# Row means by one accumulating VectorE instruction in a kernel that subtracts the mean and squares

## The chip, the cores and the metric

One core of a Trainium2 chip. The experiments ran on three such chips; each was timed in the same rounds as the kernel before, whose median was 83.1 to 83.2 us on all of them. The metric is the device time of one execution in microseconds (us). All runs were at a granted clock of 1.0. Times given are medians of several executions; a ratio is the mean time of one kernel's runs over that of the kernel before in the same rounds, so it is not quite the ratio of the two medians. The span of a profile, 81.4 us for the kernel before, is shorter than the time by some 1.8 us. A transfer is issued when the instruction that hands it to the queue starts, and has landed when the last of its 16 completion signals arrives; between landing and the first instruction that waited for it lie some 0.02 us, and the text uses either. The lead of a store is the time between its issue and the landing of the transfer ahead of it.

## The reference

```python
x = randn(1024, 4096) as float32
mean = np.mean(x, axis=-1, keepdims=True)
out  = ((x - mean) ** 2).astype(np.float32)
```

16.78 MB are read and 16.78 MB written. Each element is used for one sum, one subtraction and one product.

## The kernel before

Two tiles (i = 0, 1), each of 128 partitions x 4 rows x 4096 columns, 8.39 MB. Both loads are issued at the start. Per tile ScalarE takes the mean of row 3, VectorE those of rows 0 to 2; ScalarE squares three rows and 9/16 of another, VectorE the rest; then one store, on the same queue as the loads.

```python
    for i in range(ntiles):
        x_tile = io.tile([P, Q * D], F32)
        nc.sync.dma_start(out=x_tile, in_=x_t[i])            # load 0, load 1
        tiles.append(x_tile)
    # ... cut: helpers
    #   mean_on_act: activation(Identity, scale=-inv_d, accum_out=neg_mean)
    #   mean_on_dve: reduce_sum(negate=True), then tensor_scalar_mul by inv_d
    #   square_on_act: activation(Square, bias=neg_mean), in place
    for i in range(ntiles):
        row = [tiles[i][:, q * D:(q + 1) * D] for q in range(Q)]
        m3 = mean_on_act(row[3])
        m0 = mean_on_dve(row[0])
        square_on_act(row[3], m3)
        m1 = mean_on_dve(row[1])
        square_on_act(row[0], m0)
        m2 = mean_on_dve(row[2])
        square_on_act(row[1], m1)
        square_on_act(row[2][:, :H], m2)                     # H = 9/16 of a row
        back = row[2][:, H:]
        nc.vector.tensor_scalar_add(out=back, in0=back, scalar1=m2)
        nc.vector.tensor_mul(out=back, in0=back, in1=back)
        nc.sync.dma_start(out=out_t[i], in_=tiles[i])        # store 0, store 1
```

## Time and profile before

| What | Kernel before |
|---|---|
| time, 3 runs before the prediction | 83.25 us (83.16 to 83.27) |
| span of the profile | 81.4 us |
| VectorE, ScalarE busy | 33.4 us, 34.7 us |
| transfer queue busy | 96.0% of the span |
| loads land at | 22.7 and 42.05 us |
| stores issued at | 39.68 and 59.00 us |
| stores land at | about 61.4 and 80.7 us |

### The profile page before, as it was taken

The numbers are of one execution on the slowest core, as the hardware profiler recorded it, in microseconds if no ns is written. First come the engines' busy times: TensorE is split into PE (matmuls) and PEld (weight loads), VectorE is DVE, ScalarE is ACT, GpSimd is POOL, SyncE is SP. The second block draws the span as 40 slices with busy tenths as digits, with TensorE's granted clock in tenths as the row PEclk, the third lists the DMA queues.
The fourth block names the chain that finished last, engine by engine and source line by source line (L and its number), as shares of the span: only waits on it lengthen the run. The fifth ranks groups of instructions, "written<-read, shape, count | busy, mean of one in ns | idle before, by whom it ended". The sixth has DMA issues, their size and how long they took to land.

```text
span 81.4 us, 79 instructions
## 1 busy us (share of the span) xinstructions
DVE 33.4 (41%) x16; ACT 34.7 (43%) x13; POOL 0.2 (0%) x4
## 2 busy tenths in 40 slices
DVE  0000000000089999999439999999900000000000
ACT  6000000000089999999339999999800000000000
POOL 0000000000000000000000000000000000000000
DMA  9099956999982999992999992999997499998390
GB/s 483 32 515 515 483 258 290 515 515 515 515 386 129 515 515 515 515 451 129 451 515 515 515 483 129 418 515 515 515 515 322 193 515 515 515 515 386 161 483 0
DMA packets 577, 33.55 MB, mean 412 GB/s; under 512 B 65, under 2 KB 65, under 8 KB 65
## 3 DMA queue, kind: packets, MB, share of 16 engines
q1 hardware_dynamic: 576, 33.55, 96.0%
q14 instruction: 1, 0.00, 0.0%
HBM read 16.78 MB, written 16.78 MB: 412 GB/s over the span
## 4 chain that ended last, share of the span: by engine, by line
DMA 50%; DVE 21%; SPq 0%; issue 0%
DMA x_tile<-in_x_dram 50%; DVE neg_sum L62 16%; DVE x_tile L85 2%; DVE x_tile L84 1%; DVE neg_mean L65 1%; SPq L46 0%
## 5 line engine op out<-in xcount | busy, mean ns | idle before, releaser
L62 DVE TENSOR_REDUCE neg_sum<-x_tile 128x1 f32<-128x4096 f32 x6 | 26.5, 4413 | 25.2 <-DMA x_tile<-in_x_dram 25.2
L69 ACT ACTIVATE x_tile<-x_tile,neg_mean 128x4096 f32<-128x4096 f32 (+1 forms) x8 | 26.0, 3323 | 0.1
L54 ACT ACTIVATE copy<-x_tile 128x4096 f32<-128x4096 f32 x2 | 7.2, 3617 | 23.3 <-DMA x_tile<-in_x_dram 23.3
L85 DVE TENSOR_TENSOR x_tile<-x_tile 128x1792 f32<-128x1792 f32 x2 | 4.1, 2026 | 0.1
L84 DVE TENSOR_SCALAR x_tile<-x_tile,neg_mean 128x1792 f32<-128x1792 f32 x2 | 2.3, 1154 | 0.1
L54 ACT ACT_TABLE_LOAD x1 | 1.3, 1283 | 0.7 <-PEq L103 0.7
L65 DVE TENSOR_SCALAR neg_mean<-neg_sum 128x1 f32<-128x1 f32 x6 | 0.9, 154 | 0.2
L54 ACT ACTIVATION_READ_ACCUMULATOR copy<-x_tile 128x1 f32 x2 | 0.4, 187 | 0.0
L103 POOL MEMSET const-bfloat16-1.0<- 128x1 bf16 x1 | 0.1, 101 | 0.0
L103 POOL MEMSET const-uint8-127<- 128x1 uint8 x1 | 0.1, 101 | 0.0
L103 POOL MEMSET const-float32-0.0<- 128x1 f32 x1 | 0.1, 98 | 0.2 <-issue 0.2
L103 POOL MEMSET const-float32-1.0<- 128x1 f32 x1 | 0.1, 98 | 0.0
## 6 DMA issues: line engine op xcount, KB each, us to landing
x_tile<-in_x_dram SPq DMA_DIRECT2D x2, 31.4
out_dram<-x_tile SPq DMA_DIRECT2D x2, 21.7
```

The costliest lines, as they stand in the source:

```text
L54: nc.scalar.activation(out=copy, in_=row, func=ACT.Identity, scale=-inv_d, accum_out=neg_mean)
L62: inorder(nc.vector.reduce_sum(out=neg_sum, in_=row, axis=mybir.AxisListType.X, negate=True))
L65: inorder(nc.vector.tensor_scalar_mul(out=neg_mean, in0=neg_sum, scalar1=inv_d))
L69: inorder(nc.scalar.activation(out=part, in_=part, func=ACT.Square, bias=neg_mean, scale=1.0))
L84: nc.vector.tensor_scalar_add(out=back, in0=back, scalar1=m2)
L85: nc.vector.tensor_mul(out=back, in0=back, in1=back)
L103: nc = _bacc.Bacc("TRN2", target_bir_lowering=False, num_devices=1)
```

## The change

Its intent: less VectorE time per mean. One instruction adds the left half of a row to its right half (2048 pairs), scales and accumulates, and so gives minus the mean directly. ScalarE no longer takes means, and VectorE squares only 1/8 of every fourth row.

```diff
-        m3 = mean_on_act(row[3])
-        m0 = mean_on_dve(row[0])
-        square_on_act(row[3], m3)
         ... (all means and squares of the tile)
+        for q in range(Q):
+            row = tiles[i][:, q * D:(q + 1) * D]
+            pairs = scratch.tile([P, HALF], F32)
+            neg_mean = stats.tile([P, 1], F32)
+            inorder(nc.vector.tensor_tensor_reduce(
+                out=pairs, in0=row[:, :HALF], in1=row[:, HALF:],
+                scale=-inv_d, scalar=0.0, op0=ADD, op1=ADD, accum_out=neg_mean))
+            cut = D if q < Q - 1 else LAST                   # LAST = 7/8 of a row
+            nc.scalar.activation(out=row[:, :cut], in_=row[:, :cut],
+                                 func=ACT.Square, bias=neg_mean, scale=1.0)
+            if cut < D:
+                rest = row[:, cut:]
+                nc.vector.tensor_scalar_add(out=rest, in0=rest, scalar1=neg_mean)
+                nc.vector.tensor_mul(out=rest, in0=rest, in1=rest)
         nc.sync.dma_start(out=out_t[i], in_=tiles[i])
```

More of the change, by code (lines that the diff above doesn't have):

```diff
@@ L12 @@
 ACT = mybir.ActivationFunctionType
+ADD = mybir.AluOpType.add
 @with_exitstack
@@ L30 @@
     Q = 4
-    H = D * 9 // 16
+    HALF = D // 2
+    LAST = D - D // 8
     assert B % (P * Q) == 0
@@ L40 @@
     scratch = ctx.enter_context(tc.tile_pool(name="scratch", bufs=1))
-    stats = ctx.enter_context(tc.tile_pool(name="stats", bufs=2 * ntiles * Q))
+    stats = ctx.enter_context(tc.tile_pool(name="stats", bufs=ntiles * Q))
     tiles = []
@@ L49 @@
     inorder = tc.keep_in_program_order
-    def mean_on_act(row):
-        copy = scratch.tile([P, D], F32)
-        neg_mean = stats.tile([P, 1], F32)
-        nc.scalar.activation(
-            out=copy, in_=row, func=ACT.Identity, scale=-inv_d, accum_out=neg_mean
-        )
-        return neg_mean
-    def mean_on_dve(row):
-        neg_sum = stats.tile([P, 1], F32)
-        neg_mean = stats.tile([P, 1], F32)
-        inorder(nc.vector.reduce_sum(
-            out=neg_sum, in_=row, axis=mybir.AxisListType.X, negate=True
-        ))
-        inorder(nc.vector.tensor_scalar_mul(out=neg_mean, in0=neg_sum, scalar1=inv_d))
-        return neg_mean
@@ L68, in square_on_act @@
-    def square_on_act(part, neg_mean):
-        inorder(nc.scalar.activation(
-            out=part, in_=part, func=ACT.Square, bias=neg_mean, scale=1.0
-        ))
-    for i in range(ntiles):
-        row = [tiles[i][:, q * D:(q + 1) * D] for q in range(Q)]
-        m3 = mean_on_act(row[3])
-        m0 = mean_on_dve(row[0])
-        square_on_act(row[3], m3)
-        m1 = mean_on_dve(row[1])
-        square_on_act(row[0], m0)
-        m2 = mean_on_dve(row[2])
-        square_on_act(row[1], m1)
-        square_on_act(row[2][:, :H], m2)
-        back = row[2][:, H:]
-        nc.vector.tensor_scalar_add(out=back, in0=back, scalar1=m2)
-        nc.vector.tensor_mul(out=back, in0=back, in1=back)
+    for i in range(ntiles):
+        for q in range(Q):
[3 more added lines that the diff above has]
+            inorder(nc.vector.tensor_tensor_reduce(
+                out=pairs,
+                in0=row[:, :HALF],
+                in1=row[:, HALF:],
+                scale=-inv_d,
+                scalar=0.0,
+                op0=ADD,
+                op1=ADD,
+                accum_out=neg_mean,
+            ))
+            cut = D if q < Q - 1 else LAST
+            nc.scalar.activation(
+                out=row[:, :cut],
+                in_=row[:, :cut],
+                func=ACT.Square,
+                bias=neg_mean,
+                scale=1.0,
+            )
+            if cut < D:
+                rest = row[:, cut:]
+                nc.vector.tensor_scalar_add(out=rest, in0=rest, scalar1=neg_mean)
+                nc.vector.tensor_mul(out=rest, in0=rest, in1=rest)
```

## The prediction

Passages that no trace or run shows are cut from the text below, and the cuts are marked. Some were terms of its sum, estimates: how the time of the new instruction was reckoned (some 2.3 us, which with 0.154 us for the read makes the 2.45 us a row), the 1.2 us for the tail of 512 columns, and a delay of up to 0.25 us behind the table load, without which store 0 comes at 39.4 rather than "39.4 to 39.7". With them the sum came to 11.0 us a tile for VectorE and 14.1 for ScalarE, both stores issued 0 to 0.3 us earlier, and 83.2 us. In the half-rate rival, where the instruction takes about twice as long (some 4.4 us), the 18.3 us for four rows is such a term too. That rival was the prediction's main doubt, as the trace of the kernel before has no instruction that accumulates over two inputs. The prediction set the product against it, which took 2026 ns for 1792 pairs, 1.13 ns a pair; the reduction beside it took 4413 ns for 4096 single values, 1.08 ns a value.

> **What bounds the kernel now.** I read the page first, then time order, then the waits. The kernel moves 16.78 MB in and 16.78 MB out in four transfers of 8.39 MB: load 0, load 1, store 0, store 1. The page says how busy everyone is:
>
> ```profile
> DVE 33.4 (41%) x16; ACT 34.7 (43%) x13; POOL 0.2 (0%) x4
> ...
> q1 hardware_dynamic: 576, 33.55, 96.0%
> ...
> HBM read 16.78 MB, written 16.78 MB: 412 GB/s over the span
> ```
>
> Each computing engine rests more than half of the 81.4 us span, while the transfer queue is busy 96% of it. A busy share is an average over stages, so I cut the span at the times when transfers land: 22.7 and 42.05 (the first compute of each tile starts there, having waited for a load), then 61.4.
>
> ```profile
> 22.70:42.05 19.35, 16.71 (x8) 16.72 (x6) 0.00 (x0) 1.00 1.00 434
> 42.05:61.40 19.35, 16.71 (x8) 16.72 (x6) 0.00 (x0) 1.00 1.00 434
> ```
>
> The columns are the stretch, its length, DVE, ACT and POOL busy time, PE clock, DMA share, GB/s. In both stretches each engine needs 16.7 us, the transfers need all 19.35 us, and their rate is the same 434 GB/s. In the first stretch load 1 moves while tile 0 is computed; in the second store 0 moves while tile 1 is computed. So compute lies beside a transfer both times.
>
> What matters is when the stores are issued, which is where compute could hold up the queue:
>
> ```profile
> 39.68 19.67 SPq L86 DMA_DIRECT2D out_dram<-x_tile  x2
> ...
> 42.05 3.62 ACT L54 ACTIVATE copy<-x_tile 128x4096 f32<-128x4096 f32 x1 [2.59 <-DMA x_tile<-in_x_dram]
> ...
> 45.80 13.01 ACT L69 ACTIVATE x_tile<-x_tile,neg_mean 128x4096 f32<-128x4096 f32 x4
> ...
> 56.91 2.03 DVE L85 TENSOR_TENSOR x_tile<-x_tile 128x1792 f32<-128x1792 f32 x1
> 59.00 0.34 SPq L86 DMA_DIRECT2D out_dram<-x_tile  x1
> ```
>
> Store 0 is issued at 39.68 us, 2.4 us before load 1 lands. Store 1 is issued at 59.00. The view of the transfers gives 21.6 to 21.7 us from issue to landing for a store, so store 0 lands at about 61.4 and store 1 at about 80.7. Store 0 thus lands 19.35 us after load 1, and store 1 lands 19.3 us after store 0: the pure streaming time of 8.39 MB, with no room for a gap. Each store is in the queue before the one ahead of it has drained. The chain of work that ended last lists VectorE between 42.05 and 59.0, but it follows what released the last issue. It doesn't say that the issued transfer then waited about 2.4 us for its turn. **The transfers bound every stage: four times 19.35 us is 77.4, about 3.3 us of start come ahead (load 0 lands at 22.7 rather than 19.35) and 0.7 of ending after 80.7, which makes the 81.4.**
>
> [...] The trace has a load of 1283 ns and 3698 for the squares.
>
> ```profile
> L85 DVE TENSOR_TENSOR x_tile<-x_tile 128x1792 f32<-128x1792 f32 x2 | 4.1, 2026 | 0.1
> L84 DVE TENSOR_SCALAR x_tile<-x_tile,neg_mean 128x1792 f32<-128x1792 f32 x2 | 2.3, 1154 | 0.1
> L62 DVE TENSOR_REDUCE neg_sum<-x_tile 128x1 f32<-128x4096 f32 x6 | 26.5, 4413 | 25.2 <-DMA x_tile<-in_x_dram 25.2
> L69 ACT ACTIVATE x_tile<-x_tile,neg_mean 128x4096 f32<-128x4096 f32 x6 | 21.8, 3698 | 0.1
> L69 ACT ACTIVATE x_tile<-x_tile,neg_mean 128x2304 f32<-128x2304 f32 x2 | 4.4, 2200 | 0.0
> L65 DVE TENSOR_SCALAR neg_mean<-neg_sum 128x1 f32<-128x1 f32 x6 | 0.9, 154 | 0.2
> ```
>
> **The change, part by part (per tile of four rows).**
> - **VectorE.** Removed: three reductions of 4413 ns, three scalings of 154 and the square of 1792 columns (1154 + 2026), 16.9 us. Added: four instructions over 2048 pairs. [...] The instruction order of the changed kernel shows a second, 128x1 instruction after each, which writes the accumulator; I take 154 ns from the 128x1 row. That is 2.45 us a row, 9.8 us for four. [...] Sum 11.0 us: VectorE saves 5.9.
> - **ScalarE.** Removed: the mean of 3.62 us and its accumulator read of 0.19. Added: the square of the third row grows from 2304 to all 4096 columns, and that of the fourth shrinks to 3584. A column costs (3698-2200)/1792 = 0.836 ns, so 3584 cost 3.27 us. The group of four took 13.01 us where its singles sum to 13.29, so joints overlap by 0.28; after: 3 x 3.698 + 3.27 - 0.28 = 14.1 us. Before it was 13.01 + 3.75 of mean = 16.76.
> - **The path to store 1.** Load 1 lands at 42.03. First mean at 42.05 + 2.45 = 44.5. A new mean every 2.45 us is faster than a square every 3.6, so ScalarE never waits again: end at 44.5 + 14.1 = 58.6. VectorE is done by about 53.1. Store 1 is issued at about 58.7 instead of 59.0, 0.3 us earlier, because ScalarE now idles for 2.45 us at the start of the tile, where it used to take a mean.
> - **Tile 0** gives the same: 22.7 + 2.45 + 14.1 = 39.3, store 0 at about 39.4 instead of 39.68. The order shows one thing more: ScalarE's table load, without a wait before, now stands behind the wait for load 0. It runs from 22.7 to 24.0[...], so store 0 at 39.4 to 39.7.
> - **Sum.** Transfers, sizes and queue are untouched; both stores are issued 0 to 0.3 us earlier into a queue that has 2.4 us of other work ahead. **Expected gain: none.** Any gap that I can't see is under 0.1 us. The time stays at 83.2 us.
>
> **Rivals.**
> - **The accumulating instruction runs at half rate[...].** [...] Tile 0: last mean at 22.7 + 18.3 = 41.0, last square ends at 44.3, store 0 issued at about 44.3, after load 1 landed at 42.03: the queue runs dry. A transfer into an idle queue takes about 22.0 us (load 0: issued 0.73, landed 22.7), so store 0 lands at 66.3 instead of 61.4. Tile 1 starts on VectorE after tile 0's tail at 42.2: last mean 60.5, store 1 issued at 63.8, 2.5 us ahead of 66.3, so it lands 19.35 later at 85.7. That is +5 us: 88 us, slower by 6%. [...] Against: [...]an author who had measured half rate would have had little reason for this instruction.
> - **VectorE or ScalarE had been the bound and the saved 5.9 us show.** Then the end would follow 58.7 and lie 0.3 us earlier, 82.9 us. For it: the chain of waits lists VectorE for 21%. Against: landings exactly one streaming time apart. Even then it is within 2%.
> - **The stores become too late for another reason** (the moved table load, a costlier accumulator read). An added 0.3 us per row delays only the first mean of a tile, as the later ones run ahead of the squares; the lead of 2.4 us swallows it. Same time.
>
> **Range and chances.** The stream fixes 83.2 us; three runs of the kernel before spread over 0.1 us. I give 82.9 to 83.6 for 8 in 10: 0.3 below for an unseen gap, 0.4 above for a delay that eats the lead. About 9 in 100 for the half-rate case, which would fall outside; faster by 2% would need fewer bytes, 1 in 100.
>
> **What would show it right or wrong.** The new instruction near 2.3 us (near 4.4 is the rival). VectorE busy 22 us in all instead of 33.4, ScalarE some 30 (14.4 a tile and the table load). Store issues near 39.5 and 58.7. The stretch from 42.05 to 61.4 again at 434 GB/s, and the last landing near 80.7. Wrong would be: a stretch below 434 GB/s after load 1 has landed, or a store issued later than the transfer ahead of it drains.

## The result and the profile after

83.31 us (83.19 to 83.77, 6 runs) against 83.23 us (83.16 to 83.27, 6 runs): ratio 1.0021, interval 0.9997 to 1.0044. The same time, with a hint of slower. Note the spread: 0.6 us after, 0.1 us before.

The page of the changed kernel, busy times, queue, and the chain by engine:

```profile
DVE 20.8 (25%) x20; ACT 29.4 (36%) x9; POOL 0.2 (0%) x4
...
q1 hardware_dynamic: 576, 33.55, 95.8%
...
DMA 50%; ACT 13%; ACTq 4%; DVE 3%; SPq 0%; issue 0%
```

VectorE is busy 12.6 us less and ScalarE 5.3 us less, and the queue is as full as before. In the chain, VectorE falls from 21% to 3% and ScalarE, which was not in it, takes its place (ACTq is ScalarE's sequencer). Neither share was worth any time: the chain ends with the work that released the last *issue*, and the transfer issued then still had to wait for its turn (issued at 58.53, it landed 22.2 us later; a store in an empty queue landed 20.8 us after its issue in the run with 4096 columns below).

The same two stretches as in the prediction, changed kernel:

```profile
22.70:42.05 19.35, 10.38 (x10) 15.36 (x5) 0.00 (x0) 1.00 1.00 434
42.05:61.40 19.35, 10.38 (x10) 14.08 (x4) 0.00 (x0) 1.00 1.00 434
```

Less work on both engines beside the same 434 GB/s. In time order, changed kernel:

```profile
39.22 19.65 SPq L79 DMA_DIRECT2D out_dram<-x_tile  x2
42.09 2.29 DVE L57 CUSTOM_DVE_ANT_0 pairs<-x_tile 128x2048 f32<-128x2048 f32 x1 [8.76 <-DMA x_tile<-in_x_dram]
...
44.42 14.08 ACT L68 ACTIVATE x_tile<-x_tile,neg_mean 128x4096 f32<-128x4096 f32 x4 [5.23 <-DVE neg_mean L57]
```

Both stores go out 0.5 us earlier (39.22 for 39.68, and 58.53 for 59.00), and both need 22.2 us to land where they had needed 21.6 to 21.7. The half microsecond has moved from the engines to the wait in the queue. The groups of the changed kernel, shapes kept apart:

```profile
L68 ACT ACTIVATE x_tile<-x_tile,neg_mean 128x4096 f32<-128x4096 f32 x6 | 21.8, 3698 | 6.2 <-DVE neg_mean L57 6.2
L57 DVE CUSTOM_DVE_ANT_0 pairs<-x_tile 128x2048 f32<-128x2048 f32 x8 | 18.3, 2292 | 31.7 <-DMA x_tile<-in_x_dram 31.5
L68 ACT ACTIVATE x_tile<-x_tile,neg_mean 128x3584 f32<-128x3584 f32 x2 | 6.5, 3266 | 0.0
L68 ACT ACT_TABLE_LOAD x1 | 1.3, 1283 | 22.8 <-DMA x_tile<-in_x_dram 22.8
L57 DVE DVE_READ_ACCUMULATOR2_ANT neg_mean<- 128x1 f32 x8 | 0.7, 82 | 0.0
```

The new instruction takes 2292 ns for 2048 pairs, 1.12 ns a pair, near the 2.3 us that the prediction asks for. Its 31.7 us of idle time before it look alarming and cost nothing: VectorE waits for loads.

### The profile page after: what moved, and what is told of

Read it like the earlier page. It is cut to its first block, busy times and chain, and to the rows that moved or that the text cites. A ratio compares the mean times of both kernels' runs of the same rounds, so it can differ in the third digit from the quotient of the medians.

```text
span 81.5 us, 81 instructions
## 1 busy us (share of the span) xinstructions
DVE 20.8 (25%) x20; ACT 29.4 (36%) x9; POOL 0.2 (0%) x4
## 4 chain that ended last, share of the span: by engine, by line
DMA 50%; ACT 13%; ACTq 4%; DVE 3%; SPq 0%; issue 0%
DMA x_tile<-in_x_dram 50%; ACT x_tile L68 13%; ACTq L110 4%; DVE pairs L57 3%; SPq L48 0%; DVE neg_mean L57 0%
## 5 line engine op out<-in xcount | busy, mean ns | idle before, releaser
L68 ACT ACTIVATE x_tile<-x_tile,neg_mean 128x4096 f32<-128x4096 f32 (+1 forms) x8 | 28.2, 3590 | 6.2 <-DVE neg_mean L57 6.2
L57 DVE CUSTOM_DVE_ANT_0 pairs<-x_tile 128x2048 f32<-128x2048 f32 x8 | 18.3, 2292 | 31.7 <-DMA x_tile<-in_x_dram 31.5
L68 ACT ACT_TABLE_LOAD x1 | 1.3, 1283 | 22.8 <-DMA x_tile<-in_x_dram 22.8
L78 DVE TENSOR_TENSOR x_tile<-x_tile 128x512 f32<-128x512 f32 x2 | 1.4, 693 | 0.1
L77 DVE TENSOR_SCALAR x_tile<-x_tile,neg_mean 128x512 f32<-128x512 f32 x2 | 1.0, 486 | 0.1
L57 DVE DVE_READ_ACCUMULATOR2_ANT neg_mean<- 128x1 f32 x8 | 0.7, 82 | 0.0
## 6 DMA issues: line engine op xcount, KB each, us to landing
out_dram<-x_tile SPq DMA_DIRECT2D x2, 22.2
```

The costliest lines, as they stand in the source:

```text
L57: inorder(nc.vector.tensor_tensor_reduce(out=pairs, in0=row[:, :HALF], in1=row[:, HALF:], scale=-inv_d, scalar=0.0, op0=ADD, op1=ADD, accu ...
L68: nc.scalar.activation(out=row[:, :cut], in_=row[:, :cut], func=ACT.Square, bias=neg_mean, scale=1.0,)
L77: nc.vector.tensor_scalar_add(out=rest, in0=rest, scalar1=neg_mean)
L78: nc.vector.tensor_mul(out=rest, in0=rest, in1=rest)
```

## The experiments

The theory is the prediction's: the transfers bound every stage, and the engines' time is hidden. Four runs test it from both sides: no compute at all, twice the VectorE work, and a last store held back by two amounts. The run without compute came out against it; the other eight follow that up, and measure where the slack of a late store ends.

**1. No compute.** Is the time really that of the transfers? The edit:

```diff
     for i in range(ntiles):
-        for q in range(Q):  ... all means and squares
         nc.sync.dma_start(out=out_t[i], in_=tiles[i])
```

> The kernel after the change without any compute: the two loads and the two stores alone, in the same tiles, on the same queue (the result is wrong on purpose: x itself). Theory, the transfers bound every stage: nothing changes, 83.2 us within 0.2, stores still land one streaming time (19.35 us) apart, although they are issued at about 22.7 and 42.1 us rather than 39.2 and 58.5. Rival, the engines' work on SBUF or the late issue of the stores costs the stream something: faster, 82.5 us or less.

Measured: 84.50 us, ratio 1.016 (1.0135 to 1.0184). Slower than either kernel, though it does less. Neither the theory nor its rival foretold this: taking the engines' work away gained nothing, and something else costs time. Runs 6 to 12 show that it is the *early issue*. Store 0 went out at 22.80 us; load 1 landed at 43.37 instead of 42.05; after that everything ran at the old rate. The packet records put the loss in one place. Each transfer is 8 batches of 16 packets of 64 KB, one packet for each DMA engine, 2.42 us a batch. Only the last batch of load 1 is long, 3.70 us at the median, apart from the very first batch of load 0, which took 3.0 to 3.2 us in every run, the kernel before included.

**2 to 4. Store 1 held back.** How much of the lead of a store is slack? At the end of the last tile ScalarE copies columns onto themselves:

```diff
+        if i == ntiles - 1:
+            late = row[:, :1024]        # 2048; for 4096: row 2 of the tile
+            nc.scalar.activation(out=late, in_=late, func=ACT.Identity, scale=1.0)
         nc.sync.dma_start(out=out_t[i], in_=tiles[i])
```

> The kernel after the change with one more ScalarE instruction at the end of the last tile, an Identity in place over 1024 columns, some 1.05 us (0.833 ns a column and 0.2): store 1 is issued at about 59.6 instead of 58.5 us, still 1.8 us before store 0 lands at 61.4. Theory of the prediction (the whole time until the store ahead has landed is slack): no change, 83.3 us. Rival (a store needs 22.0 us from issue to landing however early it is, as load 0 did, so that only some 0.3 us of the lead is slack): the last landing moves to 59.6 + 22.0 = 81.6, and the time to about 84.1 us.

Measured: 83.45 us, ratio 1.0035. Store 1 was issued at 59.5 and landed 21.1 us later, at 80.6: no later than before. The Identity took 1.06 us (1057 ns; 629 at 512 columns in run 7, 1909 at 2048), 0.83 ns a column and 0.2 us. The rival, 22.0 us from issue to landing whatever happens, is refuted.

> The same with an Identity over 4096 columns, some 3.6 us: store 1 is issued at about 62.2 us, 0.8 us after store 0 has landed, so the queue runs dry. With the 22.0 us of a transfer in an idle queue it lands at 84.2, 3.5 us later than now: 86.8 us. If a store in an idle queue took only its streaming time of 19.35 us, it would land at 81.6 and the time would be 84.1 us.

Measured: 85.52 us, ratio 1.0282, between the two numbers. Store 1, issued at 62.03, landed 20.8 us later. So a store in an empty queue needs 20.8 us, 1.45 more than its streaming time; the packet records show 0.85 us from issue to the first packet and 0.4 from the last packet's end to the landing. Two windows show it, first with 1024 columns, then with 4096 (no packet starts in the second):

```profile
60.00:62.50 2.50, 0.00 (x0) 0.00 (x0) 0.00 (x0) 1.00 0.98 419
```

```profile
60.00:62.50 2.50, 0.00 (x0) 2.00 (x1) 0.00 (x0) 1.00 0.00 0
```

The rule that comes out: **a store lands at the later of 19.35 us after the transfer ahead of it and 20.8 us after its own issue.** By it the harmless limit for store 1 is 61.4 + 19.35 - 20.8 = 59.95 us, an estimate. It was tested between the two:

> The changed kernel with an Identity over 2048 columns at the end of the last tile, some 1.9 us: store 1 issued at about 60.4 us. By the rule from the runs with 1.06 and 3.6 us (a store lands at the later of 19.35 us after the transfer ahead and 20.8 us after its issue) the latest harmless issue is 61.4 + 19.35 - 20.8 = 59.95 us, so it lands 0.45 us late: 83.7 us. If all of the time until store 0 has landed were slack: 83.2 to 83.3 us.

Measured: 84.00 us, ratio 1.0096. Store 1 went out at 60.51 and landed 20.8 us later, at 81.3, which is 0.55 us after 80.75. The time is 0.56 us above the 83.44 of the changed kernel in the same rounds. My 83.7 was reckoned from a base of 83.2 and an issue 0.1 us earlier; the rule holds.

**5. Twice the mean.** What the half-rate rival of the prediction would have cost, and whether compute is hidden whatever its size:

```diff
+            for again in range(2):
                 inorder(nc.vector.tensor_tensor_reduce( ... accum_out=neg_mean))
```

> The kernel after the change with each mean instruction run twice, which is what the half-rate rival of the prediction would have cost: 4.67 us a row (twice the 2.33 from start to start). Tile 0: last mean at 22.8 + 18.7 = 41.4, last square ends at 44.7, store 0 issued at about 44.8, lands at 66.5 to 66.8. Tile 1: VectorE starts at 42.6, last mean 61.3, store 1 issued at about 64.7, lands between 85.9 (store 0 plus 19.35) and 86.7 (issue plus 22.0). So 88.4 to 89.2 us, against the 88 of the prediction's rival. If VectorE's work were hidden whatever its size: 83.3 us.

Measured: 87.67 us, ratio 1.0541. Store 0 was issued at 44.55 and landed 20.7 us later, store 1 was issued at 64.3 and landed 20.8 us later, at 85.1. So the hiding has an end, at about the place that the rule says; the expectation was high because it took 22.0 us for an empty queue.

**6. No compute, but store 0 late.** Run 1 suggested that issuing a store early costs something. This run differs from it only in when store 0 goes out, apart from the copies that delay it:

```diff
+        if i == 0:
+            for a, z in ((0, D), (D, 2 * D), (2 * D, 3 * D), (3 * D, 4 * D), (0, 2944)):
+                part = tiles[i][:, a:z]
+                nc.scalar.activation(out=part, in_=part, func=ACT.Identity, scale=1.0)
         nc.sync.dma_start(out=out_t[i], in_=tiles[i])
```

> The kernel without compute again, but store 0 held back by five ScalarE copies of tile 0 onto itself until about 39.7 us (22.8 + four of 3.6 + one of 2.7), as late as in the kernel before; store 1 still goes out as soon as load 1 has landed. Theory A, formed from the run without compute (84.5 us, where the last sixteen packets of load 1 took 3.7 us instead of 2.4): a store that is put in the queue long before the load ahead of it has drained costs the queue about 1.3 us where it turns from loading to storing. Then holding it back gives the time back: 83.2 us. Rival B, something else of a kernel without compute costs the 1.3 us (idle engines, store 1 issued early too): 84.5 us again.

Measured: 83.16 us, ratio 1.0004 (0.9989 to 1.0019); store 0 at 39.28. Theory A holds. The five copies keep ScalarE busy while load 1 moves, so this run alone doesn't exclude that idle engines cost the time. The packet records speak against that: batches 2 to 8 of load 0 took 2.42 us at the median in every run, with both engines idle, and in run 9, where nothing computes, only the batch ahead of the first store is long (again apart from the very first). Store 1 still went out at 41.9, some 18 us before its first packet at 60.3, and cost nothing: a store queued early behind a *store* is harmless; a store behind a load is not (run 1, ratio 1.016).

**7. The changed kernel with store 0 later**, by one Identity at the end of tile 0:

```diff
+        if i == 0:
+            late = row[:, :512]
+            nc.scalar.activation(out=late, in_=late, func=ACT.Identity, scale=1.0)
```

> The kernel after the change with one more ScalarE Identity in place over 512 columns at the end of tile 0, some 0.65 us: store 0 is issued at about 39.85 instead of 39.2 us, 2.2 us before load 1 lands, and still before the latest harmless moment, which I work out as 42.05 + 19.35 - 20.8 = 40.6 us (20.8 us from issue to landing of a store in an empty queue, from the run with a late store 1). Theory A: 83.2 us, and the runs as close together as those of the kernel before (83.1 to 83.3), rather than up to 83.8. Rival, the spread of the changed kernel has nothing to do with when store 0 is issued: 83.3 with runs up to 83.8.

Measured: 83.13 us (83.00 to 83.29), ratio 1.0000 (0.9983 to 1.0017), store 0 at 39.59. More work, and no longer slower than the kernel before. (The changed kernel itself was timed in other rounds, so the two are compared by their ratios.)

**8. Both engines end together.** What balance would recommend: more of the fourth row for VectorE.

```diff
-    LAST = D - D // 8
+    LAST = D * 3 // 8
```

> The kernel after the change with 5/8 rather than 1/8 of every fourth row squared on VectorE, so that both engines end a tile together: VectorE 9.34 + 1.55 + 2.82 = 13.7 us, ScalarE 25.1 + 3 x 3.6 + 1.5 = 37.4, store 0 issued at about 37.5 us, 1.7 earlier than in the changed kernel and two batches of packets before load 1 ends. Theory A: some of the 1.3 us shows, 83.5 to 84.5 us, and the last batch of load 1 takes more than 2.42 us. Transfers bound and the time of the issue is indifferent as long as it is early (the prediction): 83.2 us.

Measured: 84.14 us, ratio 1.0128 (1.0108 to 1.0149). Slower by better balance. The 2560 columns on VectorE took 1554 and 2826 ns. Its time order shows the issue at 37.41 and, 0.8 us late, the first work of tile 1:

```profile
37.41 0.35 SPq L79 DMA_DIRECT2D out_dram<-x_tile  x1
42.90 2.29 DVE L57 CUSTOM_DVE_ANT_0 pairs<-x_tile 128x2048 f32<-128x2048 f32 x1 [6.47 <-DMA x_tile<-in_x_dram]
```

**9. Stores on a queue of their own.** Do loads and stores share one limit, and does another queue avoid the turn?

```diff
-        nc.sync.dma_start(out=out_t[i], in_=tiles[i])      # without compute
+        nc.scalar.dma_start(out=out_t[i], in_=tiles[i])
```

> The two loads on the first queue and the two stores on ScalarE's own queue, without compute (wrong on purpose): store 0 moves from 22.8 us on together with load 1. If the rate of 434 GB/s is one for both directions together: the same 83 to 84.5 us, load 1 lands up to 19 us later, at some 60. If loads and stores do not share the limit: load 1 lands at about 42 and store 0 at about 43, store 1 at about 63, and the time is 65 us.

Measured: 84.04 us, ratio 1.0142. Load 1 landed at 59.8 us (1.17 + 58.6), as it now shared the engines with store 0: one limit for both directions together, 437 GB/s from 42.05 to 61.40 us where one direction alone had 434. The two queues by share of the engines' time:

```profile
q1 hardware_dynamic: 288, 16.78, 49.1%
q10 hardware_dynamic: 288, 16.78, 47.1%
```

The loss is there too, once, right where stores begin (one batch of packets, the second after load 0, ended 0.94 us late, and no other did). So a second queue is no way round. After that the packets of the two queues alternated, a batch of stores and a batch of loads in turn from 27.5 to 58.9 us, and each of these batches took 2.42 us: the change between loading and storing as such cost nothing that shows. What costs, as far as these runs show, is the first store that arrives while loads are under way.

**10 to 12. Where the harm begins.** The changed kernel unedited, and two with LAST in between:

```diff
-    LAST = D - D // 8
+    LAST = D - D // 4          # last_3072;   D * 5 // 8 in last_2560
```

> The changed kernel unedited, timed again beside the kernel before and beside the next three. Its store 0 is issued at 39.2 us, where the sixteen last packets of load 1 start between 38.56 and 39.32 us. If the early issue touches it, its runs spread up to 83.5 to 83.8 us and the mean is 0.2 to 0.3% above that of the kernel before; if the 0.2% of the first comparison was chance, 83.2 us and a ratio of 1.000.

Measured: 83.44 us (83.33 to 83.72), ratio 1.0032 (1.0014 to 1.0050). Clear of noise now: the changed kernel is slower by 0.2 to 0.3%. In its profile store 0 went out at 39.12, and some of load 1's last packets took up to 2.73 us, so that load 1 landed at 42.23, 0.2 us later than in the kernel before, though load 0 had been no later.

> The changed kernel with 2/8 rather than 1/8 of every fourth row on VectorE: ScalarE ends 0.43 us earlier, store 0 is issued at about 38.8 us, after the first of load 1's last packets have started and before the rest. Theory A in its finer form (what costs is a store that is known to a DMA engine before that engine starts its last load packet): a part of the 1 us, 83.3 to 84.0 us. If the issue must precede the last packets clearly to cost anything: 83.2 us.

Measured: 83.77 us, ratio 1.0068. The issue came at 38.54, earlier than I had worked out and just ahead of the first of the last packets; the last batch took 3.07 us at the median.

> The same with 3/8 of every fourth row on VectorE: store 0 issued at about 38.35 us, 0.2 us before the first of load 1's last packets starts. Finer theory A: if an issue takes effect within 0.2 us the full 1 us, 84.1 us as with an issue at 37.4; if it takes some 0.8 us to reach the DMA engines (a store into an empty queue issued at 62.04 had its first packet start at 62.88), then it comes too late for most engines, 83.2 to 83.6 us.

Measured: 84.09 us, ratio 1.0101, issue at 38.19. The full loss, though by the 0.85 us of an empty queue the store's packets would not have started before 39.0 (an estimate, 38.19 + 0.85), when most of load 1's last packets were under way. So the second branch of that expectation is refuted: it is not needed that the store's own packets be ready before the last load packets start.

The runs on one queue in which neither store came late, by the time of store 0's issue (issue and last column are from one profiled execution each; last column: median of the 16 last packets of load 1):

| Kernel | Store 0 issued | Time | Ratio | Last batch of load 1 |
|---|---|---|---|---|
| no compute | 22.80 | 84.50 | 1.0160 | 3.70 us |
| balanced, LAST 3/8 | 37.41 | 84.14 | 1.0128 | 3.24 |
| LAST 5/8 | 38.19 | 84.09 | 1.0101 | 3.11 |
| LAST 6/8 | 38.54 | 83.77 | 1.0068 | 3.07 |
| changed kernel, again | 39.12 | 83.44 | 1.0032 | 2.43, up to 2.73 |
| changed kernel | 39.22 | 83.31 | 1.0021 | 2.43 |
| no compute, held | 39.28 | 83.16 | 1.0004 | 2.43 |
| changed, tile 0 later | 39.59 | 83.13 | 1.0000 | 2.42 |
| kernel before | 39.68 | 83.2 | 1 | 2.43 |

One window tells it, 40.5 to 42.0 us, in which the first packets of store 0 should start. Its last two columns count the packets that start in it, with their whole duration (so the share can pass 1) and their data. Kernel before:

```profile
40.50:42.00 1.50, 0.00 (x0) 0.00 (x0) 0.00 (x0) 1.00 1.63 699
```

LAST 6/8:

```profile
40.50:42.00 1.50, 0.00 (x0) 0.00 (x0) 0.00 (x0) 1.00 1.21 524
```

LAST 5/8:

```profile
40.50:42.00 1.50, 0.00 (x0) 0.00 (x0) 0.00 (x0) 1.00 0.91 393
```

Balanced:

```profile
40.50:42.00 1.50, 0.00 (x0) 0.00 (x0) 0.00 (x0) 1.00 0.40 175
```

No compute (this kernel has no columns for the engines that it doesn't use):

```profile
40.50:42.00 1.50, 0.00 (x0) 1.00 0.00 0
```

No compute, store 0 held (no VectorE column):

```profile
40.50:42.00 1.50, 0.00 (x0) 0.00 (x0) 1.00 1.62 699
```

The earlier store 0 is issued, the fewer of its packets have begun by 42 us. The amount of compute doesn't order the table: kernels without means and squares stand at its top and near its bottom, and the changed kernel stands lower with one instruction more. No version that beats the kernel before was found. From about 39.3 us on the issue of store 0 is free, up to 39.68 at least, where the kernel before lies already; nothing between that and 44.55 was tried. The rule for store 1 would put the end at 40.6 us (42.05 + 19.35 - 20.8, an estimate), but the packet records of the kernel before make an earlier one likely: put in order of time, 14 of the 16 first packets of store 0 start 0.05 to 0.15 us after the last load packets end, the first of them 1.46 us after the issue, where the empty queue took 0.85. In the changed kernel there is no such gap. So the kernel before already lies near the late end of a narrow stretch.

## Why the prediction was right

- **Transfers bound, no gain expected**: right. 83.2 predicted, 83.31 and 83.44 measured, 83.2 for the kernel before.
- **The new instruction near 2.3 us**: 2292 ns. The half-rate rival, near 4.4, did not come true (the product that was set against it reads the same columns twice, in0 and in1 alike, so it was weaker evidence than it looked), and run 5 shows that it would have cost 4.4 us or a little less (the prediction had 5, from an empty-queue transfer of 22.0 instead of 20.8 us).
- **The accumulator read at 154 ns**: 82. A row from start to start takes 2.33 us instead of 2.45, and VectorE 10.38 us a tile instead of 11.0.
- **ScalarE 14.1 us a tile**: 14.08. The "some 30" us in all at the prediction's end took 14.4 a tile, without the overlap of its own sum; measured 29.4.
- **The moved table load**, for which the prediction allowed a delay: it cost nothing. It ended at 24.11 us, and the first square began at 25.11, 0.03 us after the accumulator read that gave its mean.
- **Store issues at 39.4 to 39.7 and 58.7**: 39.22 and 58.53, earlier because the accumulator read was shorter and the table load cost nothing.
- **"a queue that has 2.4 us of other work ahead"**: this step failed, without moving the time here. Only part of the 2.4 us is slack. Store 1 of the kernel before, issued at 59.00, could be 0.95 us later (limit 59.95), not 2.4.
- **An earlier issue is free**: the other failed step, implied in the sum. Nothing was gained by it, and for store 0 something was lost. From 39.3 us back to 38.2 the cost rises to about 0.9 us, and with an issue at 22.8 to 1.3. How much of the step from 0.9 to 1.3 us is due to the issue and how much to the missing compute was not separated. The changed kernel lies on the edge of that. This accounts for the 0.3% of its second timing, whose profile shows the lengthened packets, and run 7, which moved store 0 by 0.37 us, was no slower than the kernel before; in the profile of the first comparison (a run of 83.31 us) no packet at the turn was longer than 2.44 us, so for its 0.2% and its run of 83.77 us it is the likely cause and not a shown one.
- **Partly luck**: the prediction gave no limit for an early issue. Had the change freed ScalarE of 1.8 us more, as run 8 did, the time would have been about 84.1 us, outside its range of 82.9 to 83.6.

**What stays open** is the mechanism of the loss at the turn. The runs show where it is (the last load packets, when a store was issued while much of the last batch was still to go), that it is paid once, that it follows the issue time and not the amount of compute, and that a second queue has one too. A cost of every change from reading to writing is ruled out: the kernel before turns without a loss, and in run 9 loads and stores alternate at 2.42 us a batch. What takes the time there, they do not show.

## What to carry to other kernels

When landings follow each other at exactly one streaming time, faster engines have nothing to give (here landings 19.35 us apart, and no gain from 12.6 us less work on VectorE and 5.3 on ScalarE); compare landing distances before shares of busy time, and don't take an engine's share of the chain that ended last for time to be won. The slack of an issue is its lead less the extra time that a transfer in an empty queue needs (here 1.45 us for store 1), not the whole lead; measure it by delaying the issue on purpose. And an issue can also be too early (here one at 38.19 us cost about 0.9 us): where one queue turns from loads to stores, look at the packets around the turn before balancing the engines further.
